# Three more pairs of up projections in seven products, their sums of x by way of DRAM, and no pair held across the two phases

## Chip, core and metric

One core of a Trainium2 chip. The metric is the device time of one execution in microseconds; the kernel before took 696.33 us as the median of three runs (696.13 to 696.6).

## What is computed

One block of an encoder on x of 512 positions by 1024 features, all in float32. The part that matters here is the channel mixer at its end; ahead of it stand a projection, a gated convolution, attention over 8 heads, and their merge through two gates and w_o, which gives a new x.

```python
h = rms_norm(x, norm_ffn_g[l])
up = causal_dwconv(h @ w_up[l], conv_ffn_w[l])      # 1024 -> 2 x 2816, three taps
a, b = jnp.split(up, 2, axis=-1)
x = x + (jax.nn.silu(a) * b) @ w_down[l]            # 2816 -> 1024
...
return rms_norm(x, norm_f_g)
```

## The kernel before

**Layout.** Features lie on the partitions and the 512 positions along the free axis, so x is 8 blocks of 128 x 512. The 2816 hidden features are 22 blocks; block j of a and block j of b are together pair j (blocks up 2j and 2j + 1 of `wup`).

**Products.** Each float32 operand is split into a high part and the remainder (`wh`, `wl` of a weight, `xh`, `xl` of an activation), and a product is three matmuls: high by high, low by high, high by low (`mm3`, L308; `passes`, L326, in an order of its own: first all that need only `wh`, then those with `wl`). Every matmul of the mixer takes 128 x 128 weights and 256 columns. The split of a chunk of weights is `split` (L274 on ScalarE makes `wh`, L278 on VectorE makes `wl`); there are two buffers of each, so the split of a chunk can begin when TensorE has finished the chunk before the current one.

**Two by two steps.** Some products are done on 2 x 2 arrangements of 128 x 128 weight blocks and of 256-column halves of two activation blocks, with seven products in place of eight (`PROD`, `seven`). The seven need sums of the weight blocks and sums of the activation blocks, and their results are put together by additions. A step handles two such arrangements and has two chunks of weights: P (blocks as they are, 768 columns, 18 matmuls) and F (four sums, 1024 columns, 24 matmuls). The sums of weights are made in DRAM: `make_forms` lists copies on SyncE's queue and adding transfers on GpSimd's queue, and `slot()`, called at places in the program, issues those whose turn it is. The forms for a group are made some 20 us ahead.

**Where they are used.** The gates (`GATES`), three up pairs (`SUP = (1, 2, 5)`), and the down projection (`STEPS`). For the up pairs, `up_forms(q)` makes the sums of two blocks of x in a single buffer `y` (four arrays of 128 x 256): `scale` (L1048, L1051, L1052), `sums` (L1055, L1056), `parts_of` (L1059, L1060), which splits y into slots 26 to 41 of `gh` and `gl`. This runs during the eight blocks of w_o (L1079 to L1081), whose squares GpSimd adds up in `ssq` (L1002); TensorE takes `ssq` (`pc_n`, L343) in the middle of the first up blocks.

**Phases.** The mixer runs in two phases (`PHASES`): up pairs 0 to 11 and a down stage of 12 steps, then up pairs 12 to 21 and a down stage of 8 steps with a rest done plainly. A plain up block is one chunk of 1024 columns and 48 matmuls. `up` evacuates it by a scaling (L1141), three taps (L561, L562, L565) and, per pair, `glu`: Silu (L1201), a product on GpSimd (L1206 for even pairs, L1213 for odd ones), then for two pairs together sums (L1223 to L1228) and splits (L1232, L1233) into `gh` and `gl`. A pair of seven products is put together by `merge` (L1162 to L1184) ahead of the taps, a pair of output blocks by `combine` (L1252 to L1271). In phase 0's down stage output pairs 0, 1 and 3 are combined; pair 2 stays open in four PSUM banks (`HELD = 2`) through phase 1's up stage, whose plain blocks therefore take turns in the other four.

**Order.** Matmuls, DMA issues and GpSimd's products stand in program order. The additions, scalings and splits of activations wait in a list (`later`) and are let out behind each split of weights, each with a cost and a due chunk (`run_later`), or are forced where something needs a bank or an operand (`flush`). Raw weights are loaded up to seven chunks ahead by SyncE's queue (`load`, four buffers for `raw`, four for F chunks).

Of the kernel before, what the change touches and what calls it, by code (L numbers as in the profile page):

```python
# [13 lines left out]
P = 128  # L14
# [39 lines left out]
HELD = 2  # L54
# [11 lines left out]
N0 = len(GATES) + len(UPD)  # L66
GROUPS = {"gate": (2, 4, 1), "up": (2, 4, 1), 0: (2, 4, 1), 1: (2, 3, 1)}
# [3 lines left out]
def block_kernel(ctx, tc, xT, vecs, wv, win, wmix, wo, wup, wst, wdp, outT):  # L71
# [70 lines left out]
    for ph, (j0, j1) in enumerate(PHASES):  # L142
        for j in range(j0, j1):
            if j in SUP:
# [45 lines left out]
    def make_forms(n0, n1, key):  # L190

        size, step, shift = GROUPS[key]
        make_forms.slot = 0
# [4 lines left out]
        for g, (a, b) in enumerate(zip(cuts, cuts[1:])):  # L198
# [15 lines left out]
            todo_bg.extend((make_forms.slot + step * k + shift * g, op) for k, op in enumerate(ops))  # L214
# [571 lines left out]
    def seven(doubles, n0, sets, operand, goes_on=None, stays=None, done=None, of="q"):  # L786
# [14 lines left out]
        for n, (name, prods) in enumerate(todo):  # L801
            wh, wl = chunk(name)
# [4 lines left out]
            for c, i, (xh, xl), b, h in prods:  # L807
                if i not in open_:
# [5 lines left out]
                    (i, b) not in before and i != goes_on, (i, b) not in after and i != stays,  # L814
                ))
            passes(out, len(out))
            if name[0] == "F":
                for i in sorted({i for _, i, *_ in prods}):
                    if (i, 0) not in after and i != stays:
                        done(i, open_.pop(i), sets[i])  # L820
# [125 lines left out]
    make_forms(len(GATES), N0, "up")  # L946
# [92 lines left out]
    def up_forms(q):  # L1039

        y = gx.tile([P, 4, 2 * P], F32, tag="y", name=f"y{q}")
        b11, b12, b21, b22 = (y[:, i, :] for i in range(4))
        fs = slice(XF + 4 * q, XF + 4 * q + 4)
# [13 lines left out]

        def parts_of():
            nc.scalar.activation(gh[:, fs, :], y, AF.Copy)  # L1059
# [5 lines left out]
    def up_form(q, g):  # L1065
# [3 lines left out]
        n = XF + 4 * q + (0, 3, 1, 2)[g - 3]  # L1069
# [3 lines left out]
    make_forms(N0, N0 + len(STEPS[0]), 0)  # L1073
    for j in range(KB):
# [11 lines left out]
        if j % 2:  # L1086
            up_forms(j // 2)
# [20 lines left out]
    USETS = {1: (2, 3, 4, 5), 2: (6, 7, 0, 1), 5: (6, 7, 0, 1)}  # L1108
    ssq3 = xp.tile([P, S], F32, tag="ssq", name="ssq3")

    def place(ph, q):
        return (q - PHASES[ph][0] // 2) * (NF + ph)

    def up(j, ph, rb2, pu=None):
# [6 lines left out]

        if j in SUP:
            c = len(GATES) + 2 * SUP.index(j)
            slot()
            seven(
                UPD[c - len(GATES) :][:2], c, {j: USETS[j]}, up_form, of="x",
# [166 lines left out]
    for ph, (j0, j1) in enumerate(PHASES):  # L1293
        if ph:
            flush()
            acc = turns(*X * 5)
        if ph:
            make_forms(N0 + len(STEPS[0]), len(DOUBLES), ph)
        for j in range(j0, j1):
# [11 lines left out]
            up(j, ph, nrm["b"], pu)  # L1311
        assert not todo_bg
        flush((("e",),))
        seven(
            STEPS[ph], N0 + ph * len(STEPS[0]), ({0: X, 1: Y, 3: X, 2: Y}, {0: X, 1: Y, 2: Y})[ph],
            lambda q, g: (gh[:, place(ph, q) + g, :], gl[:, place(ph, q) + g, :]),
            goes_on=HELD if ph == 1 else None, stays=HELD if ph == 0 else None,
            done=lambda i, banks, ids: combine(ph, i, banks, ids),
        )
# [95 lines left out]
def _layout(i):  # L1415
# [46 lines left out]
    for w4, d in [(wga, d) for d in GATES] + [(wu4, d) for d in UPD] + [(wdn, d) for d in STEPS[0] + STEPS[1]]:  # L1462
# [45 lines left out]
```

## Time and profile before

| | |
|---|---|
| median of 3 runs | 696.33 us (696.13 to 696.6) |
| profiled execution | 695.75 us, of which the span from the first to the last instruction is 693.9 us |
| mean granted TensorE clock | 0.998 |
| SyncE's and ScalarE's DMA (q1 and q10) | 42016 packets, 100.87 MB |
| GpSimd's DMA (q0) | 16304 packets, 22.88 MB |

Times in a row of the profile are microseconds from the span's start. PE is TensorE, PEld its weight loads, DVE VectorE, ACT ScalarE, POOL GpSimd, SPq SyncE's DMA queue. A row of the timeline reads: start, length, engine, line, operation, output and inputs, shape, count, and in brackets the engine's idle time before it with what ended it. A row of the groups by line gives count, busy time and the mean of one in ns. A row of waits gives the sum, the number and the longest. An operation that follows another on the same engine can begin a little before the other's end; the distance between starts is what it costs in a row of work.

### The profile page before, as it was taken

How to read it: one execution, taken by the hardware profiler on the slowest of the kernel's cores; microseconds unless marked ns; L12 is line 12 of the kernel's file. 1: busy time of each engine (PE TensorE's matmuls, PEld its weight loads, DVE VectorE, ACT ScalarE, POOL GpSimd, SP SyncE). 2: the span in 40 equal slices, each digit the busy share in tenths (PEclk: the TensorE clock that was granted, in tenths of full speed). 3: DMA queues.
4: the chain of work that ended last, by engine and by line, in shares of the span. 5: the costliest groups of instructions: out<-in, count | busy, mean ns of one | idle time of the engine just before them, and what ended most of it. 6: DMA issues, size and time to landing. Idle time of an engine off the chain costs nothing.

```text
span 693.9 us, 14635 instructions
## 1 busy us (share of the span) xinstructions
PE 686.2 (99%) x5972; PEld 684.6 (99%) x5972; DVE 531.4 (77%) x826; ACT 359.2 (52%) x565; POOL 178.3 (26%) x194
## 2 busy tenths in 40 slices
PE   9999999999999999999999999999999999999996
PEld 9999999999999999999999999999999999999996
DVE  6677877776577778768879799888774677777894
ACT  5665655644565444446554455545443344445572
POOL 4134846532221201113513134210000313222000
PEclk9999999999999999999999999999999999999999
DMA  7528988543698596766899776355646686776513
GB/s 256 158 70 272 197 200 193 129 91 92 223 263 244 166 269 193 207 217 141 114 316 294 201 178 135 116 177 176 201 128 232 141 195 157 188 169 172 164 31 122
DMA packets 58387, 124.68 MB, mean 180 GB/s; under 512 B 5280, under 2 KB 26800, under 8 KB 58320
## 3 DMA queue, kind: packets, MB, share of 16 engines
q1 hardware_dynamic: 40776, 99.68, 44.5%
q0 software_dynamic: 16304, 22.88, 20.9%
q10 hardware_dynamic: 1240, 1.19, 0.5%
q8 instruction: 47, 0.77, 0.4%
q14 instruction: 20, 0.16, 0.1%
HBM read 121.57 MB, written 39.32 MB: 232 GB/s over the span
## 4 chain that ended last, share of the span: by engine, by line
PE 96%; DVE 3%; issue 0%; ACT 0%; DVEq 0%
PE dn L326 24%; PE p_up L308 21%; PE p_in L308 14%; PE p_up L326 6%; PE p_wo L308 6%; PE yc L308 3%; PE ya L308 3%; PE pa L472 2%; PE pb L474 2%; PE p_q L308 2%; PE p_k L308 2%; PE p_gb L308 2%; PE p_ga L308 2%; PE o L653 2%; PE tp L636 1%; PE pdB L308 1%
## 5 line engine op out<-in xcount | busy, mean ns | idle before, releaser
L308 PE MATMUL p_up<-x1h,wh_up 128*128 128x256 f32 x464 | 90.5, 276 | 0.0
L308 PE MATMUL p_up<-x1h,wl_up 128*128 128x256 f32 x464 | 90.4, 276 | 0.0
L308 PE MATMUL p_up<-x1l,wh_up 128*128 128x256 f32 x464 | 90.3, 276 | 0.0
L308 PEld LDWEIGHTS p_up<-x1h,wh_up 128*128 128x128 f32 x464 | 69.9, 188 | 0.0
L308 PEld LDWEIGHTS p_up<-x1h,wl_up 128*128 128x128 f32 x464 | 69.9, 188 | 0.0
L308 PEld LDWEIGHTS p_up<-x1l,wh_up 128*128 128x128 f32 x464 | 69.8, 188 | 0.0
L274 ACT ACTIVATE wh_up<-raw_up 128x1024 fp32r<-128x1024 f32 x38 | 40.2, 1057 | 49.6 <-PE p_up L308 43.0
L210 POOL DMA_DIRECT2D f<-in_wst_dram x57 | 65.5, 1309 | 0.1
L278 DVE TENSOR_TENSOR wl_F<-raw_F,wh_F 128x1024 fp32r<-128x1024 f32 (+1 forms) x36 | 47.8, 1328 | 18.5 <-ACT wh_F L274 18.2
L308 PE MATMUL p_in<-xgh,wh_in 128*128 128x256 f32 x288 | 56.8, 279 | 0.0
L308 PE MATMUL p_in<-xgh,wl_in 128*128 128x256 f32 x288 | 56.6, 278 | 0.0
L308 PE MATMUL p_in<-xgl,wh_in 128*128 128x256 f32 x288 | 56.5, 278 | 0.0
L278 DVE TENSOR_TENSOR wl_up<-raw_up,wh_up 128x1024 fp32r<-128x1024 f32 x38 | 47.1, 1240 | 12.1 <-ACT wh_up L274 12.1
L274 ACT ACTIVATE wh_F<-raw_F 128x1024 fp32r<-128x1024 f32 (+1 forms) x36 | 37.9, 1053 | 35.4 <-PE dn L326 27.8
L1206 POOL TENSOR_TENSOR ge<-fu,fu 128x512 f32<-128x512 f32 x11 | 18.8, 1706 | 141.6 <-DVE fu L565 117.6
L274 ACT ACTIVATE wh_P<-raw_P 128x768 fp32r<-128x768 f32 (+1 forms) x36 | 30.0, 834 | 31.6 <-PE dn L326 22.3
L278 DVE TENSOR_TENSOR wl_P<-raw_P,wh_P 128x768 fp32r<-128x768 f32 (+1 forms) x36 | 35.0, 972 | 13.7 <-ACT wh_P L274 9.1
L308 PEld LDWEIGHTS p_in<-xgh,wh_in 128*128 128x128 f32 x288 | 44.7, 188 | 0.7
L326 PE MATMUL dn<-gl,wh_F 128*128 128x256 f32 x192 | 45.1, 276 | 0.0
L326 PE MATMUL dn<-gh,wh_F 128*128 128x256 f32 x192 | 45.1, 276 | 0.0
L308 PEld LDWEIGHTS p_in<-xgl,wh_in 128*128 128x128 f32 x288 | 43.7, 188 | 0.0
L308 PEld LDWEIGHTS p_in<-xgh,wl_in 128*128 128x128 f32 x288 | 43.6, 188 | 0.0
(349 smaller groups left out, 2148.5 us busy)
## 6 DMA issues: line engine op xcount, KB each, us to landing
raw_up<-in_wup_dram SPq DMA_DIRECT2D x38, 512.0 KB, 4.2
raw_F<-f SPq DMA_DIRECT2D x35, 512.0 KB, 4.5
raw_P<-in_wst_dram SPq DMA_DIRECT2D x35, 384.0 KB, 4.9
raw_in<-in_win_dram SPq DMA_DIRECT2D x26, 512.0 KB, 3.5
f<-in_wst_dram POOLq DMA_DIRECT2D x35, 256.0 KB, 6.4
f<-in_wst_dram SPq DMA_DIRECT2D x17, 512.0 KB, 5.7
f<-in_wst_dram POOLq DMA_DIRECT2D x17, 512.0 KB, 8.0
f<-f SPq DMA_DIRECT2D x34, 256.0 KB, 5.4
```

The source lines that it names most:

```text
L210: return lambda: keep(nc.gpsimd.dma_start(dst, src, accum_op=ALU.add))
L274: ins = nc.scalar.activation(hi, raw, AF.Copy)
L278: ins = nc.vector.tensor_sub(lo, raw, hi.bitcast(F32))
L308: keep(nc.tensor.matmul(out[:, cs], w, x[:, cs], start=start and i == 0 and c == 0, stop=stop and i == 2 and c == len(cut) - 1,))
L326: keep(nc.tensor.matmul(out, wl if x == 1 else wh, xl if x == 2 else xh, start=opens and bk not in seen, stop=closes and bk not in left,))
L472: keep(nc.tensor.matmul(pa[t][:, :VW], xt, w[:, VB:], start=start, stop=stop))
L474: keep(nc.tensor.matmul(pb[t], xt, w[:, :VB], start=start and t % 2 == 0, stop=stop and t % 2 == 1))
L636: keep(nc.tensor.transpose(tp[:, ks], pt[:, ks], ident))
L653: keep(nc.tensor.matmul(o[:, 2 * P * e + c0 : 2 * P * (e + 1)], w, x[:, kb, c0:], start=e == 0 and kb == 0 and i == 0, stop=e == 1 and kb ...
L1206: keep(nc.gpsimd.tensor_mul(ge, a.rearrange(halves_of, h=2), b.rearrange(halves_of, h=2)))
```

## The change

Pairs 14, 16 and 18 of phase 1 are done in seven products as well. `SUP`, `UPD` and `XF` become lists by phase. The sums of x for them are the same as those for pairs 1, 2 and 5, but their slots of `gh` and `gl` are used by other data in between: so `parts_of` stores each `y` to a DRAM array `ys` on ScalarE's queue in phase 0, and `up_forms(q, 1)` loads it again on SyncE's queue into the same single buffer and splits it a second time, one q behind each split from the last but one chunk of phase 0's down stage on, into slots 0 to 15. The places of phase 1's products in `gh` and `gl` move to leave these slots free. The sums of weights for the three pairs are listed from slot 20 on beside those of the down stage, and `seven` calls `slot()` in the down stage too. Pair 2 is no longer held: it is combined in both phases, and phase 1's plain blocks and pairs of seven products use all eight banks.

```diff
-SUP = (1, 2, 5)
-XF = 26
-UPD = tuple(((j, q), (j, q + 1)) for j in SUP for q in (0, 2))
-DOUBLES = GATES + UPD + STEPS[0] + STEPS[1]
+SUP = ((1, 2, 5), (14, 16, 18))
+XF = (26, 0)
+UPD = tuple(tuple(((j, q), (j, q + 1)) for j in js for q in (0, 2)) for js in SUP)
+DOUBLES = GATES + UPD[0] + STEPS[0] + UPD[1] + STEPS[1]
+NU = [len(GATES), len(GATES + UPD[0] + STEPS[0])]
+ND = [NU[i] + len(UPD[i]) for i in range(2)]
...
-    def seven(doubles, n0, sets, operand, goes_on=None, stays=None, done=None, of="q"):
+    def seven(doubles, n0, sets, operand, done=None, of="q", tick=False):
...
+            if tick and name[0] == "P":
+                slot()
...
-                    (i, b) not in before and i != goes_on, (i, b) not in after and i != stays,
+                    (i, b) not in before, (i, b) not in after,
...
-    def up_forms(q):
-
-        y = gx.tile([P, 4, 2 * P], F32, tag="y", name=f"y{q}")
+    ys = dr.tile([4, P, 4, 2 * P], F32, tag="ys", name="ys")
+
+    def up_forms(q, ph):
+
+        y = gx.tile([P, 4, 2 * P], F32, tag="y", name=f"y{ph}{q}")
...
         def parts_of():
             nc.scalar.activation(gh[:, fs, :], y, AF.Copy)
+            if not ph:
+                keep(nc.scalar.dma_start(ys[q], y))
             nc.vector.tensor_sub(gl[:, fs, :], y, gh.bitcast(F32)[:, fs, :])
-
+            if ph and q < 3:
+                up_forms(q + 1, ph)
+
+        if ph:
+            keep(nc.sync.dma_start(y, ys[q]))
+            due = [c[0] for c in stream].index(f"F{ND[0] + len(STEPS[0]) - 2}") + q
+            later.append((due, 0.85, (("x", q),), parts_of))
+            return
...
-    make_forms(N0, N0 + len(STEPS[0]), 0)
+    make_forms(ND[0], ND[0] + len(STEPS[0]), 0)
+    make_forms(NU[1], ND[1], "up1", 20)
...
-    USETS = {1: (2, 3, 4, 5), 2: (6, 7, 0, 1), 5: (6, 7, 0, 1)}
+    USETS = dict.fromkeys(SUP[1], (2, 3, 4, 5)) | {1: (2, 3, 4, 5), 2: (6, 7, 0, 1), 5: (6, 7, 0, 1)}
...
     def place(ph, q):
-        return (q - PHASES[ph][0] // 2) * (NF + ph)
+        return (16, 24, 32, 0, 8)[q - PHASES[1][0] // 2] if ph else q * NF
...
         if ph:
-            flush()
-            acc = turns(*X * 5)
-        if ph:
-            make_forms(N0 + len(STEPS[0]), len(DOUBLES), ph)
+            acc = turns(6, 7, 0, 1, 6, 7, 0, 1, 6, 7, 0, 1, 6, 7)
+            make_forms(ND[1], len(DOUBLES), ph)
...
             up(j, ph, nrm["b"], pu)
+        if not ph:
+            up_forms(0, 1)
+        flush_only((("e",),))
+        seven(
+            STEPS[ph], ND[ph], ({0: X, 1: Y, 3: X, 2: Y}, {0: X, 1: Y, 2: Y})[ph],
+            lambda q, g: (gh[:, place(ph, q) + g, :], gl[:, place(ph, q) + g, :]),
+            done=lambda i, banks, ids: combine(ph, i, banks, ids), tick=True,
+        )
         assert not todo_bg
```

The lines of the changed kernel are shifted by one at `split` (L279 is the L278 of before) and by 16 in `up` and `glu` (L1157 is L1141). Three places in the order of instructions matter. The first is ScalarE at the end of the blocks of w_o, from the split of the third y on; before it reads:

```order
L1059 ACTIVATE gh<-y_4392 128x1024
L274 ACTIVATE wh_up_4537<-raw_up_4331 128x1024
L1080 ACTIVATE x1h<-x_3803,vec 128x512
L1001 ACTIVATE sq_6_4460<-x_3803 128x512
L1048 ACTIVATE y_4525<-x_3803,vec 128x512
L274 ACTIVATE wh_up_4551<-raw_up_4394 128x1024
L1080 ACTIVATE x1h<-x_3803,vec 128x512
L1001 ACTIVATE sq_7_4522<-x_3803 128x512
```

and now:

```order
L1065 ACTIVATE gh<-y_4398 128x1024
L1067 DMA ys<-y_4398 128x1024
L275 ACTIVATE wh_up_4544<-raw_up_4337 128x1024
L1096 ACTIVATE x1h<-x_3803,vec 128x512
L1004 ACTIVATE sq_6_4467<-x_3803 128x512
L1053 ACTIVATE y_4532<-x_3803,vec 128x512
L275 ACTIVATE wh_up_4558<-raw_up_4400 128x1024
L1096 ACTIVATE x1h<-x_3803,vec 128x512
L1004 ACTIVATE sq_7_4529<-x_3803 128x512
```

Only the store is new; the scaling that writes the next y stands behind it in the queue and uses the buffer that it reads. VectorE's order in this stretch is unchanged.

The second is VectorE where phase 1's up stage ends and its down stage begins; wl_P and wl_F are the low parts of the first step's two chunks, fz the scalings of the last up blocks, go and gl the sums and splits of earlier pairs. Before:

```order
L1141 TENSOR_TENSOR fz_8139<-p_up_8090,rb_n_4669 128x512
L278 TENSOR_TENSOR wl_P_8212<-raw_P_8007,wh_P_8211 128x768
L562 SCALAR_TENSOR_TENSOR fu_8141<-fz_8139,vec,fu_8141 128x511
L565 SCALAR_TENSOR_TENSOR fu_8141<-fz_8139,vec,fu_8141 128x510
L1141 TENSOR_TENSOR fz_8215<-p_up_8158,rb_n_4669 128x512
L278 TENSOR_TENSOR wl_F_8245<-raw_F_8009,wh_F_8244 128x1024
```

Now, from the fourth instruction behind wl_P on (a tap, a scaling and a tap stand between):

```order
L1239 TENSOR_TENSOR go_8205<-ge_8004 128x256
L563 SCALAR_TENSOR_TENSOR fu_8281<-fz_8279,vec,fu_8281 128x511
L1240 TENSOR_TENSOR go_8205<-go_8205,ge_8004 128x256
L566 SCALAR_TENSOR_TENSOR fu_8281<-fz_8279,vec,fu_8281 128x510
L1243 SCALAR_TENSOR_TENSOR go_8205<-go_8205 128x256
L1157 TENSOR_TENSOR fz_8285<-p_up_8215,rb_n_4677 128x512
L1244 SCALAR_TENSOR_TENSOR go_8205<-go_8205 128x256
L1249 TENSOR_TENSOR gl<-ge_8004,gh 128x2x256
L1249 TENSOR_TENSOR gl<-go_8205,gh 128x512
L563 SCALAR_TENSOR_TENSOR fu_8287<-fz_8285,vec,fu_8287 128x511
L279 TENSOR_TENSOR wl_F_8331<-raw_F_8058,wh_F_8330 128x1024
```

Between wl_P and wl_F stood three instructions; now thirteen, since work of the blocks before has moved back to here.

The third is VectorE in pair 14, the first in seven products. Before, no such pair stood there. Now, from the split of its second P chunk on:

```order
L279 TENSOR_TENSOR wl_P_7258<-raw_P_7061,wh_P_7257 128x768
L1240 TENSOR_TENSOR go_7191<-go_7191,ge_7058 128x256
L1243 SCALAR_TENSOR_TENSOR go_7191<-go_7191 128x256
L1249 TENSOR_TENSOR gl<-ge_7058,gh 128x2x256
L1244 SCALAR_TENSOR_TENSOR go_7191<-go_7191 128x256
L279 TENSOR_TENSOR wl_F_7288<-raw_F_7063,wh_F_7287 128x1024
L1249 TENSOR_TENSOR gl<-go_7191,gh 128x512
L279 TENSOR_TENSOR wl_up_7318<-raw_up_7128,wh_up_7317 128x1024
```

The sum L1240 needs GpSimd's product of pair 13, and the low part of the second F chunk stands behind it.

More of the change, by code (lines that the diff above doesn't have):

```diff
@@ L53 @@
 )
-HELD = 2
 GJ = 3
@@ L188, in block_kernel, with make_forms @@
     made, todo_bg = {}, []
-    def make_forms(n0, n1, key):
+    def make_forms(n0, n1, key, start=0):
         size, step, shift = GROUPS[key]
-        make_forms.slot = 0
+        if not start:
+            make_forms.slot = 0
         cuts = [n0]
@@ L818, in seven @@
                 for i in sorted({i for _, i, *_ in prods}):
-                    if (i, 0) not in after and i != stays:
+                    if (i, 0) not in after:
                         done(i, open_.pop(i), sets[i])
```

32 lines of the change are left out of this document (12 added, 20 removed).

## Prediction

> **What bounds the kernel now.** The page comes first: its head line, the busy line, and the shares of the chain that ended last.
>
> ```profile
> span 693.9 us, 14635 instructions
> PE 686.2 (99%) x5972; PEld 684.6 (99%) x5972; DVE 531.4 (77%) x826; ACT 359.2 (52%) x565; POOL 178.3 (26%) x194
> PE 96%; DVE 3%; issue 0%; ACT 0%; DVEq 0%
> ```
>
> TensorE is busy 99% of the span and 96% of the chain is its own work. The list of waits says how much it waits once the first loads are in:
>
> ```profile
> PE p_up L326 <- DVE wl_up L278: 0.6, 1, 0.6
> ```
>
> So there is one wait of 0.6 us for VectorE, and the time is the number of matmuls times their spacing, as long as VectorE, ScalarE and the queues keep up. The chain in order of time gives the spacing:
>
> ```profile
> 468.15 57.12 PE dn L326 x504
> ...
> 526.63 4.08 PE p_up L308 x36
> ...
> 634.07 35.91 PE dn L326 x315
> ```
>
> 57.12 us over 504 matmuls is 0.1133 us each, and 4.08 over 36 is the same. The first row is the down stage of phase 0, which ends at 525.27. Phase 1's 20 up blocks run until 634.07; its down stage begins there. The profiled execution took 695.75 us around a span of 693.9; the median of the runs is 696.33, 0.58 above, so differences found in the span are put on the median.
>
> **The gain.** A plain pair is 2 blocks of 48 matmuls, 96; in seven products it is 84. Three pairs lose 36 matmuls of the same form: 36 x 0.1133 = **4.08 us**, all on the path. No other matmul is removed or added. What follows is what the new work puts in front of TensorE.
>
> **The stores of the sums (L1067 of the changed kernel).** ScalarE issues each store behind the split of y; since y has one buffer, the scaling of the next y now waits until the store has landed. Behind it in ScalarE's queue stand the next weight split, x1h and the square, and VectorE's sums of y wait for it too. This is the last of the three places, on ScalarE, VectorE, GpSimd and TensorE:
>
> ```profile
> 333.57 1.06 ACT L1059 ACTIVATE gh<-y 128x1024 fp32r<-128x1024 f32 x1 [2.35 <-DVE y L1056]
> 334.53 1.05 ACT L274 ACTIVATE wh_up<-raw_up 128x1024 fp32r<-128x1024 f32 x1
> ...
> 337.68 0.71 ACT L1048 ACTIVATE y<-x,vec 128x512 f32<-128x512 f32 x1
> ```
>
> ```profile
> 306.31 0.42 DVE L1051 TENSOR_TENSOR y<-y 128x256 f32<-128x256 f32 x1
> ...
> 338.42 1.31 DVE L1051 TENSOR_TENSOR y<-y 128x256 f32<-128x256 f32 x1
> 339.65 0.68 DVE L1079 TENSOR_TENSOR x<-p_wo,x 128x512 f32<-128x512 f32 x1
> ```
>
> ```profile
> 337.92 1.52 POOL L1002 TENSOR_TENSOR ssq<-ssq,sq 128x512 f32<-128x512 f32 x1 [4.67 <-ACT sq L1001]
> ...
> 341.75 1.52 POOL L1002 TENSOR_TENSOR ssq<-ssq,sq 128x512 f32<-128x512 f32 x1 [1.31 <-ACT sq L1001]
> ```
>
> ```profile
> 343.05 0.39 PE L308 MATMUL p_up<-x1l,wh_up 128*128 128x256 f32 x2
> 343.32 1.05 PE L343 MATMUL pc_n<-ones,ssq 128*128 128x1 f32 x8
> ```
>
> The store would issue at 334.53, the scaling starts at 337.68: 3.15 us are free. The sum of 1.31 is done in 0.42 elsewhere (306.31); it lasts until the GpSimd addition beside it is done (339.44). Without that collision it would free the queue after 0.34, so the scaling may start as late as 339.65 - 0.34 - 0.74 = 338.57, and a store may take 4.0 us before x (339.65) is late. From there nothing is spare: the addition ends at 343.27 and TensorE takes ssq at 343.32, straight behind its last matmul. A store of S us makes x late by S - 4.0, and since the next split of y is late by the same, three stores in a row cost TensorE 3 x (S - 4.0).
>
> No 512 KB store is in this trace. The nearest rows are the output's stores (128 and 256 KB), the loads of 512 KB in a quiet stretch (raw_up from 500 to 560), and those of this stage (raw_wo), in this order, as smallest, median, largest:
>
> ```profile
> DMA to landing us min/median/max: 1.7/2.9/3.7
> ```
>
> ```profile
> DMA to landing us min/median/max: 3.5/3.8/4.3
> ```
>
> ```profile
> DMA to landing us min/median/max: 4.2/5.1/6.5
> ```
>
> The ends are 0 (1.7) and 3 x 2.5 = 7.5 us (6.5). I take S = 4.2, nearer to the quiet load, since the stores stand in ScalarE's own queue and not behind SyncE's copies: **0.6 us**. The Trainium skill's page "DMA: Bandwidth & Descriptors", section "Anatomy of one DMA — SWDGE (gpsimd) path", gives about 2.0 us plus bytes over 436 GB/s, which as an estimate for 512 KB is 3.2 us; by it the stores cost nothing and the time would be 694.0. The same section says the receipt from HBM is the heavy part and can delay the signal surprisingly long, which speaks against this change; the loads here, above 3.2 in every row, bear the second sentence out better than the figure.
>
> **Loading the sums back.** The load of y1 waits for VectorE's split of y0; SyncE's queue holds it in front of y2 and of the load of up27, neither of which is needed before 536. ScalarE's split of y1 stands in front of that of the first up block:
>
> ```profile
> 514.88 1.07 ACT L274 ACTIVATE wh_F<-raw_F 128x1024 fp32r<-128x1024 f32 x1 [1.65 <-PE dn L326]
> ...
> 521.91 1.06 ACT L274 ACTIVATE wh_up<-raw_up 128x1024 fp32r<-128x1024 f32 x1 [1.20 <-PE dn L326]
> ```
>
> ```profile
> 515.98 1.23 DVE L278 TENSOR_TENSOR wl_F<-raw_F,wh_F 128x1024 fp32r<-128x1024 f32 x1 [0.41 <-ACT wh_F L274]
> ```
>
> y0's low part follows at 517.1 and ends at 518.3; the load at 3.8 lands at 522.2, ScalarE's split ends at 523.2, the block's two splits at 524.3 and 525.5. TensorE wants the low half eight matmuls after 525.27, at 526.2: 0.7 us to spare, 0.2 with a load of 4.3, and 1.3 late at 5.8. y2 and y3 go round the same way (about 6.2 us each) and come out some 1.9 us before up27 wants its split. Zero here.
>
> **VectorE in the new stage.** Back to back, its operations stand this far apart:
>
> ```profile
> 427.10 1.21 DVE L278 TENSOR_TENSOR wl_up<-raw_up,wh_up 128x1024 fp32r<-128x1024 f32 x1
> 428.23 0.74 DVE L562 SCALAR_TENSOR_TENSOR fu<-fz,vec,fu 128x511 f32<-128x511 f32 x1
> 428.89 0.41 DVE L1233 TENSOR_TENSOR gl<-ge,gh 128x256 fp32r<-128x256 f32 x1
> 429.23 0.74 DVE L565 SCALAR_TENSOR_TENSOR fu<-fz,vec,fu 128x510 f32<-128x510 f32 x1
> 429.89 0.68 DVE L1233 TENSOR_TENSOR gl<-go,gh 128x512 fp32r<-128x512 f32 x1
> 430.49 0.68 DVE L1141 TENSOR_TENSOR fz<-p_up,rb_n 128x512 f32<-128x512 f32 x1
> 431.09 1.28 DVE L1233 TENSOR_TENSOR gl<-go,gh 128x512 fp32r<-128x512 f32 x2
> ```
>
> 1.13 for 1024 columns, 0.66 for a tap, 0.60 for 512, 0.34 for 256. A plain pair is two splits, two scalings and four taps, 6.1, and half of the sums for the down stage (four of 256, four splits of 512, 3.8), 1.9: 8.0 us beside 10.88 of TensorE. A pair of seven products has splits of 768 (0.87) and 1024, twice, 4.0, merge and taps 6.1, and the 1.9: 12.0 us beside 9.52. Two such neighbours are 20.0 against 20.4, so VectorE only just holds from 14 to 19 and is behind at the end, where its order decides. Before, that end reads:
>
> ```profile
> 628.67 0.69 DVE L1141 TENSOR_TENSOR fz<-p_up,rb_n 128x512 f32<-128x512 f32 x1 [0.54 <-PE p_up L308]
> 629.55 0.96 DVE L278 TENSOR_TENSOR wl_P<-raw_P,wh_P 128x768 fp32r<-128x768 f32 x1 [0.19 <-ACT wh_P L274]
> ...
> 635.28 1.23 DVE L278 TENSOR_TENSOR wl_F<-raw_F,wh_F 128x1024 fp32r<-128x1024 f32 x1 [0.47 <-ACT wh_F L274]
> ```
>
> wl_F is ready 2.44 after the last block's end E (634.07); TensorE wants it after the P chunk's 18 matmuls and 16 of the F chunk's, at E + 3.85. Now wl_P can start at E - 4.52 as before (its buffer is freed by the last but one block), and 13 operations stand between it and wl_F: five taps, two scalings, four sums, two splits of 512, 3.30 + 1.20 + 1.36 + 1.20 = 7.06. With 0.87 for wl_P, wl_F starts at E + 3.41 and is ready at E + 4.64, **0.8 late**. Then a tap, two splits and the next wl_P (0.66 + 1.20 + 0.96) end at E + 7.36, where TensorE, resumed at 4.64, wants it 0.91 + 1.36 later at 6.91: **0.45 late**. After that the old slack returns.
>
> Three rows more bear on the start of the stage: VectorE's wait for the first block, its wait for GpSimd's product, and the down stage ahead of it in the table by stretches (length, then busy time and count of TensorE, its loads, VectorE, ScalarE, GpSimd, then clock, share of the DMA engines and GB/s):
>
> ```profile
> 530.75 0.69 DVE L1141 TENSOR_TENSOR fz<-p_up,rb_n 128x512 f32<-128x512 f32 x1 [4.02 <-PE p_up L308]
> ...
> 552.51 0.43 DVE L1224 TENSOR_TENSOR go<-go,ge 128x256 f32<-128x256 f32 x1 [1.46 <-POOL go L1213]
> ```
>
> ```profile
> 468.00:525.30 57.30, 57.30 (x508) 57.30 (x507) 42.58 (x57) 27.45 (x34) 0.00 (x0) 1.00 0.59 179
> ```
>
> The seven additions of pair 2's combine and the splits of y2 and y3 go into the 4.0 us ahead of the first block and the waits that follow it. The weight sums for pairs 14, 16 and 18 end in the down stage, where GpSimd did nothing and the DMA engines were busy 59%; the loads that they feed are due 22 us later. So both cost nothing, and a late sum would show as a wait for a raw tile. The tight spots are wl_up24 (0.7), the second F chunk of pair 14, which now stands behind GpSimd's product (walked through with the spacings above it is ready 30.0 us after the stage's start and wanted at 30.4), and up30 (0.4). A collision such as the 1.31 above stretches an operation by 0.9; one that lands on a tight spot costs up to 0.5. I take **0.5** for all, ends 0 and 1.5.
>
> **Sum.** -4.08 + 0.6 + 0.8 + 0.45 + 0.5 = -1.73; 696.33 - 1.73 = **694.6 us**.
>
> **Rivals.** *Nothing waits* (chance 0.18): stores within 4.0 us, and VectorE's order a little kinder than my sum: -4.08, 692.2. For it: no wait but one in the whole trace. Against it: the 7.06 us are a plain sum of rows. *The stores are late* (0.18), which ends slower: nothing else hides a landing, and every 0.1 us above 4.0 counts three times. The gain without stores is 4.08 - 1.75 = 2.33, so they cancel it from S = 4.0 + 2.33 / 3 = 4.8 on; at 5.6, within raw_wo's rows, it is 4.8 us instead of 0.6, 698.8. GpSimd's adding transfers run beside the second and third store, for it; the separate queue, against. *VectorE is overrun* (0.12): its idle time in phase 1 goes, so GpSimd's ten products meet it; at 0.5 each on four spots more, 2 us, 696.6. The Trainium skill's page "SBUF — State Buffer", section "SBUF: two separate sides", calls that port pair an exclusive lock held for the whole instruction; the 1.31 us row agrees.
>
> **Numbers.** The forecast has 0.52, its own range 693.6 to 695.8, the rest the rivals. What a measurement of this kernel can tell is about 0.2%, 1.4 us, so faster means below 694.9: 0.36 of the forecast's share and the first rival's 0.18, 0.54. Same: 0.16 of the forecast, most of the overrun (0.12) and the store case between 4.8 and 5.2 (0.03), 0.31. Slower 0.15, the rest of the stores. The range runs from the full gain, 692.2, to 697.6 (S near 5.2), leaving out late stores beyond that.
>
> **What would show it.** TensorE's matmuls fewer by 36; the waits of TensorE: pc_n on ssq near 343 by 3 x (S - 4.0), with S read from the stores' landing; dn on wl_F and then wl_P at the start of the last down stage; a small one near pair 14. Wrong would be stores beyond 5 us, or waits of TensorE on a raw tile's load.

## The result and the profile after

The changed kernel took 704.48 us (median of 4 runs, 704.01 to 705.18) against 696.41 for the kernel before on the same chip: a ratio of 1.0118, interval 1.0103 to 1.0133. It is **8.1 us slower**, where 694.6 was predicted and 697.6 was the upper end. The profiled execution took 704.37, its span is 702.6.

The head of the page after, its busy line and its chain by engine:

```profile
span 702.6 us, 14695 instructions
PE 688.5 (98%) x5936; PEld 686.2 (98%) x5936; DVE 551.7 (79%) x858; ACT 369.8 (53%) x579; POOL 190.2 (27%) x203
PE 86%; DVE 6%; DMA 4%; ACT 2%; issue 1%; POOL 0%; DVEq 0%; SPq 0%; ACTq 0%; POOLq 0%
```

The 36 matmuls are gone (5972 to 5936), yet TensorE is busy 2.3 us longer: single matmuls must have become slower. And the chain, which was 96% TensorE's own work, now runs through VectorE, DMAs and ScalarE. The list of TensorE's waits names where (sum, number, longest):

```profile
PE dn L327 <- DVE wl_F L279: 2.9, 2, 2.5
PE pc_n L344 <- POOL ssq L1005: 2.7, 1, 2.7
PE warm L115 <- DVE ones L107: 1.1, 1, 1.1
PE p_up L309 <- DVE wl_up L279: 0.6, 1, 0.6
PE p_up L327 <- DVE wl_up L279: 0.6, 1, 0.6
```

The waits for ones and one of those for wl_up were there before. New are 2.7 + 0.6 us at the first up blocks, and 2.5 + 0.4 at the last down stage and near pair 14. The table by stretches of 2 us, for both places, shows the rest. Behind the length stand busy time and count of TensorE, its loads, VectorE, ScalarE and GpSimd, then the granted clock:

```profile
346.00:348.00 2.00, 0.32 (x3) 0.32 (x3) 1.85 (x3) 0.90 (x2) 1.51 (x1) 1.00 0.82 122
348.00:350.00 2.00, 2.00 (x12) 2.00 (x12) 0.96 (x3) 1.06 (x1) 0.62 (x1) 0.55 0.73 154
350.00:352.00 2.00, 2.00 (x11) 2.00 (x11) 1.23 (x1) 0.00 (x0) 2.00 (x3) 0.50 0.78 217
352.00:354.00 2.00, 2.00 (x11) 2.00 (x11) 0.00 (x0) 0.00 (x0) 0.55 (x1) 0.50 0.82 260
354.00:356.00 2.00, 2.00 (x16) 2.00 (x15) 0.00 (x0) 0.50 (x1) 0.00 (x0) 0.74 1.04 401
642.00:644.00 2.00, 0.00 (x0) 0.00 (x0) 2.00 (x4) 1.99 (x3) 0.00 (x0) 1.00 0.00 0
644.00:646.00 2.00, 1.46 (x9) 1.46 (x10) 2.00 (x4) 2.00 (x4) 0.00 (x0) 0.79 0.19 35
646.00:648.00 2.00, 2.00 (x11) 2.00 (x11) 2.00 (x3) 0.30 (x1) 0.00 (x0) 0.50 0.57 227
648.00:650.00 2.00, 2.00 (x17) 2.00 (x16) 1.35 (x3) 0.85 (x1) 0.00 (x0) 0.86 0.50 126
```

Behind each of the two long waits TensorE is granted half its clock, for 6.8 and 3.4 us; a row of 2 us then holds 11 or 12 matmuls in place of 20. The loss is the missing share of the clock times 2 us, summed: 2 x (0.45 + 0.50 + 0.50 + 0.26) = 3.4 us and 2 x (0.21 + 0.50 + 0.14) = 1.7 us. So the span's difference of 8.7 us is -4.08 for the matmuls, +2.7 + 0.6 + 2.9 for the waits, +3.4 + 1.7 for the clock, together 7.2, and 1.5 us that the list of waits does not name (0.57 of it lies ahead of the blocks of w_o, where the change does nothing).

**The first wait** comes down ScalarE's queue. Its timeline, the splits of y and the scalings of the next y (ACTq is the issue of the store; the first two rows are the first store and the scaling behind it):

```profile
312.17 0.34 ACTq L1067 DMA_DIRECT2D ys<-y  x1
...
316.51 0.72 ACT L1053 ACTIVATE y<-x,vec 128x512 f32<-128x512 f32 x1 [0.17 <-DMA ys<-y]
...
323.16 0.33 ACTq L1067 DMA_DIRECT2D ys<-y  x1
...
329.95 0.72 ACT L1053 ACTIVATE y<-x,vec 128x512 f32<-128x512 f32 x1 [2.61 <-DMA ys<-y]
...
336.00 1.06 ACT L1065 ACTIVATE gh<-y 128x1024 fp32r<-128x1024 f32 x1 [2.37 <-DVE y L1061]
336.03 0.33 ACTq L1067 DMA_DIRECT2D ys<-y  x1
...
342.91 0.72 ACT L1053 ACTIVATE y<-x,vec 128x512 f32<-128x512 f32 x1 [2.71 <-DMA ys<-y]
```

The last two of these scalings start 6.8 and 6.9 us behind the issue of the store, and the engine sat idle 2.6 and 2.7 us for it; the first starts 4.3 us behind, and ScalarE sat idle 0.17. The store is issued while ScalarE's split of y begins (336.03, 336.00), not behind it. From there it goes on as the prediction had it: VectorE's x of the last block, GpSimd's addition, TensorE:

```profile
344.01 0.68 DVE L1095 TENSOR_TENSOR x<-p_wo,x 128x512 f32<-128x512 f32 x1
```

```profile
346.12 1.51 POOL L1005 TENSOR_TENSOR ssq<-ssq,sq 128x512 f32<-128x512 f32 x1 [3.24 <-ACT sq L1004]
```

```profile
347.68 1.42 PE L344 MATMUL pc_n<-ones,ssq 128*128 128x1 f32 x8 [2.72 <-POOL ssq L1005]
```

x stood at 339.65 before, the addition at 341.75, pc_n at 343.32: all are 4.4 us late.

**The second wait** is that of the first F chunk of the last down stage. VectorE's splits and the two long taps between, and GpSimd at the same time:

```profile
632.11 1.50 DVE L563 SCALAR_TENSOR_TENSOR fu<-fz,vec,fu 128x511 f32<-128x511 f32 x1
634.31 0.95 DVE L279 TENSOR_TENSOR wl_P<-raw_P,wh_P 128x768 fp32r<-128x768 f32 x1
635.18 0.74 DVE L563 SCALAR_TENSOR_TENSOR fu<-fz,vec,fu 128x511 f32<-128x511 f32 x1
637.43 1.78 DVE L563 SCALAR_TENSOR_TENSOR fu<-fz,vec,fu 128x511 f32<-128x511 f32 x1
...
643.27 1.22 DVE L279 TENSOR_TENSOR wl_F<-raw_F,wh_F 128x1024 fp32r<-128x1024 f32 x1
```

```profile
631.76 1.30 POOL L1229 TENSOR_TENSOR go<-fu,fu 128x512 f32<-128x512 f32 x1 [8.60 <-ACT fu L562]
637.32 1.34 POOL L1222 TENSOR_TENSOR ge<-fu,fu 128x512 f32<-128x512 f32 x1 [4.26 <-ACT fu L562]
```

A tap takes 0.74 alone, and 1.50 and 1.78 while GpSimd multiplies.

### The profile page after: what moved, and what is told of

Read it like the earlier page. It is cut to its first block, busy times and chain, and to the rows that moved or that the text cites. A ratio compares the mean times of both kernels' runs of the same rounds, so it can differ in the third digit from the quotient of the medians.

```text
span 702.6 us, 14695 instructions
## 1 busy us (share of the span) xinstructions
PE 688.5 (98%) x5936; PEld 686.2 (98%) x5936; DVE 551.7 (79%) x858; ACT 369.8 (53%) x579; POOL 190.2 (27%) x203
## 4 chain that ended last, share of the span: by engine, by line
PE 86%; DVE 6%; DMA 4%; ACT 2%; issue 1%; POOL 0%; DVEq 0%; SPq 0%; ACTq 0%; POOLq 0%
PE dn L327 26%; PE p_up L309 15%; PE p_in L309 14%; PE p_up L327 5%; PE yc L309 3%; PE ya L309 3%; DMA ys<-y 3%; PE pa L473 2%; PE pb L475 2%; PE p_q L309 2%; PE p_k L309 2%; PE p_gb L309 2%; PE p_ga L309 2%; PE o L654 2%; PE tp L637 1%; PE p_wo L309 1%
## 5 line engine op out<-in xcount | busy, mean ns | idle before, releaser
L211 POOL DMA_DIRECT2D f<-in_wst_dram x66 | 75.1, 1389 | 31.6 <-DMA f<-f 31.6
L309 PE MATMUL p_up<-x1h,wl_up 128*128 128x256 f32 x392 | 77.5, 280 | 0.6 <-DVE wl_up L279 0.6
L309 PE MATMUL p_up<-x1h,wh_up 128*128 128x256 f32 x392 | 77.7, 280 | 0.0
L309 PE MATMUL p_up<-x1l,wh_up 128*128 128x256 f32 x392 | 77.3, 279 | 0.0
L279 DVE TENSOR_TENSOR wl_F<-raw_F,wh_F 128x1024 fp32r<-128x1024 f32 (+1 forms) x42 | 55.1, 1313 | 19.3 <-ACT wh_F L275 19.3
L309 PEld LDWEIGHTS p_up<-x1h,wl_up 128*128 128x128 f32 x392 | 60.1, 191 | 0.8 <-DVE wl_up L279 0.8
L309 PEld LDWEIGHTS p_up<-x1h,wh_up 128*128 128x128 f32 x392 | 60.3, 191 | 0.0
L309 PEld LDWEIGHTS p_up<-x1l,wh_up 128*128 128x128 f32 x392 | 60.0, 191 | 0.0
L279 DVE TENSOR_TENSOR wl_P<-raw_P,wh_P 128x768 fp32r<-128x768 f32 (+1 forms) x42 | 40.8, 971 | 17.0 <-ACT wh_P L275 12.5
L327 PE MATMUL dn<-gh,wh_F 128*128 128x256 f32 x228 | 53.8, 276 | 0.0
L327 PE MATMUL dn<-gl,wh_F 128*128 128x256 f32 x228 | 53.8, 276 | 0.0
L279 DVE TENSOR_TENSOR wl_up<-raw_up,wh_up 128x1024 fp32r<-128x1024 f32 x32 | 40.9, 1278 | 6.5 <-ACT wh_up L275 6.3
```

Source lines behind the costliest of these rows:

```text
L211: return lambda: keep(nc.gpsimd.dma_start(dst, src, accum_op=ALU.add))
L279: ins = nc.vector.tensor_sub(lo, raw, hi.bitcast(F32))
L309: keep(nc.tensor.matmul(out[:, cs], w, x[:, cs], start=start and i == 0 and c == 0, stop=stop and i == 2 and c == len(cut) - 1,))
L327: keep(nc.tensor.matmul(out, wl if x == 1 else wh, xl if x == 2 else xh, start=opens and bk not in seen, stop=closes and bk not in left,))
```

## The experiments

The theory behind the first runs has three parts. A: the stores' landing, through the single buffer, costs the wait for ssq. B: VectorE is behind at the last down stage because of the third pair. C: an idle TensorE loses its clock, which doubles the price of both. The rivals are that the stores hurt by their traffic, that the wait at the end lies in the order of instructions and not in their number, and that the clock falls for another reason. The results, each as a ratio to the kernel before on the same chip:

| kernel | us | ratio, 95% interval |
|---|---|---|
| a_two_y | 697.27 | 1.0016 (1.0007 to 1.0026) |
| a_early | 705.17 | 1.0125 (1.0107 to 1.0143) |
| a_fill | 700.59 | 1.0064 (1.0049 to 1.0079) |
| b_stores | 702.88 | 1.0096 (1.0080 to 1.0111) |
| a2_budget | 702.46 | 1.0088 (1.0074 to 1.0101) |
| a2_pairs | 696.69 | 1.0014 (1.0005 to 1.0023) |
| b_slow1 | 699.03 | 1.0048 (1.0033 to 1.0063) |
| b_slow2 | 701.90 | 1.0085 (1.0072 to 1.0099) |
| a3_split | 697.69 | 1.0019 (1.0010 to 1.0028) |
| a3_split2 | 697.09 | 1.0015 (1.0006 to 1.0025) |
| a4_tbl | 694.13 | 0.9972 (0.9961 to 0.9984) |
| a2_dve2 | 696.43 | 1.0007 (0.9998 to 1.0016) |

### The stores: a_two_y and b_stores

The changed kernel with a second place for y (a_two_y):

```diff
-        y = gx.tile([P, 4, 2 * P], F32, tag="y", name=f"y{ph}{q}")
+        pool = gx if ph or q % 2 else hp
+        y = pool.tile([P, 4, 2 * P], F32, tag="y", name=f"y{ph}{q}")
```

> The changed kernel, with the sums of x for the even q in a second buffer, so that a scaling waits for the store before the last and no longer for the last one. Theory A (the stores' landing is what delays the chain from the scaling of y to ssq; TensorE then waits 2.7 us for ssq and 0.6 us for a weight split, and runs at half clock for some 7 us behind it): both waits go, the clock stays at 1.0 near 350, and the time falls from 704.5 by 2.7 + 0.6 + 3.5 = 6.8 us to about 697.7 (697 to 698.5). Rival (the stores delay the stage by their traffic, whatever buffer they read): the waits stay, 702 to 705.

The kernel before with the stores and nothing else (b_stores):

```diff
             nc.scalar.activation(gh[:, fs, :], y, AF.Copy)
+            keep(nc.scalar.dma_start(ys[q], y))
```

> The kernel before with nothing but the four stores of y added on ScalarE's queue; nobody reads what they store. Theory A: the stores alone bring the wait of 2.7 us for ssq, some 0.5 us for a split, and 3.5 us at half clock: 696.4 + 6.7 = about 703 (702 to 704). Rival (the loss at the start comes from other work that the change brings there, such as the longer list of weight sums): under 698.

Both came out as theory A said: 697.27 (expected 697.7) and 702.88 (expected 703). In a_two_y no scaling waits for a store any more, pc_n starts at 343.33 as before the change, and the table by stretches keeps the full clock:

```profile
346.00:348.00 2.00, 2.00 (x20) 2.00 (x19) 0.89 (x1) 0.02 (x1) 1.83 (x2) 1.00 0.83 197
348.00:350.00 2.00, 2.00 (x20) 2.00 (x19) 0.96 (x1) 0.83 (x1) 0.00 (x0) 1.00 1.00 390
```

The same four stores move the same bytes there, and the slowest of the transfers of ys even takes longer to land than in the changed kernel (longest 8.2 us, against 6.8). So TensorE waits because of the buffer and not because of the traffic. In b_stores, where ys is only stored, the view of that tile gives the landing without the loads among it (smallest, median, largest):

```profile
DMA to landing us min/median/max: 6.7/6.8/6.8
```

The view can tell the landing of two of the four stores only, the second and the third. The first was quicker: the scaling behind it starts 4.1 us after its issue (311.56, 315.64) and waits for nothing. What makes the difference is not shown. In the changed kernel GpSimd issues one of its adding transfers 1.4 us ahead of the second store and again ahead of the third (321.79 and 334.66) and none near the first, and the DMA engines are busy 0.68 of the stretch from the first store's issue to its landing, 0.95 and 0.87 of the other two; no run takes these transfers away.

### The clock: a_fill, b_slow1 and b_slow2

The changed kernel with idle multiplications put into the two waits (a_fill):

```diff
+    def filler(b, n):
+        t = bank(b, "fill")
+        for _ in range(n):
+            keep(nc.tensor.matmul(t[:, :P], ones, ones, start=True, stop=True))
...
                 def mid():
+                    filler(7, 11)
                     nrm["c"] =
...
-            passes(out, len(out))
+            passes(out, len(out), 10 if name == f"F{ND[1]}" else 0)
```

> The changed kernel with multiplications added whose results nobody reads: 11 matmuls of 128 columns ahead of pc_n and 10 ahead of the first that needs wl_F in the last down stage, each about 0.21 us by the first matmuls of the trace (4.21 us for 9 at half clock), so 2.3 and 2.1 us of work inside waits of 2.7 and 2.5. Theory C (the clock falls because TensorE stands idle in these two waits, and the half clock costs 3.5 and 2 us more): the granted clock stays at 1.0 in both places, the waits are filled but nothing starts earlier, and the time falls by 4.5 to 5.5 us to about 699.5. Rival (the clock falls for another cause, such as the load of the chip, or the waits alone are the loss): the clock falls as before and the time stays within 1 us of 704.5.

The kernel before with one or two operations more ahead of pc_n (b_slow1, b_slow2):

```diff
+    for _ in range(NSLOW):
+        nc.gpsimd.tensor_scalar(ssq2, ssq2, 1.0, None, op0=ALU.mult)
     hg.close()
```

> The kernel before with one more GpSimd operation of 128x512 on ssq (times 1.0), so that TensorE must wait some 1.3 us for ssq. If the clock falls with any wait: 1.3 us and some 3.5 us at half clock, 701. If a wait must be longer than this for the clock to fall: 696.3 + 1.3 = 697.6, with a granted clock of 1.0 behind it.

> The kernel before with two more GpSimd operations of 128x512 on ssq (times 1.0), so that TensorE waits some 2.7 us for ssq, with no store and no transfer added. Theory C (the idle time of TensorE alone brings the clock down): half clock for some 7 us behind the wait, 696.3 + 2.7 + 3.5 = 702.5. Rival (the stores or the load of the DMA engines near 350 bring it down): the clock stays at 1.0, 699.0.

In a_fill the work needed starts no earlier than in the changed kernel, and the time falls by 3.9 us (expected 4.5 to 5.5). TensorE's rows at the two places show the fill and what is left of the waits, and the last one a wait that the slow clock had covered:

```profile
345.19 2.72 PE L318 MATMUL fill<-ones 128*128 128x128 f32 x22
348.13 1.05 PE L352 MATMUL pc_n<-ones,ssq 128*128 128x1 f32 x8 [0.22 <-POOL ssq L1013]
...
639.32 2.39 PE L318 MATMUL fill<-ones 128*128 128x128 f32 x20
642.02 1.21 PE L335 MATMUL dn<-gh,wl_F 128*128 128x256 f32 x8 [0.30 <-DVE wl_F L279]
644.75 0.97 PE L335 MATMUL dn<-gh,wl_P 128*128 128x256 f32 x6 [0.16 <-DVE wl_P L279]
```

The granted clock is 1.00 throughout both places. So the clock is the second half of the price, and an idle TensorE is the reason. The two slowed kernels say how long idle must last. b_slow1, the wait and the stretch behind it:

```profile
345.54 1.05 PE L344 MATMUL pc_n<-ones,ssq 128*128 128x1 f32 x8 [1.53 <-POOL ssq L1090]
```

```profile
348.00:350.00 2.00, 2.00 (x20) 2.00 (x20) 0.00 (x0) 0.00 (x0) 2.00 (x3) 1.00 0.98 385
```

and b_slow2:

```profile
347.13 1.86 PE L344 MATMUL pc_n<-ones,ssq 128*128 128x1 f32 x8 [3.11 <-POOL ssq L1090]
```

```profile
348.00:350.00 2.00, 2.00 (x10) 2.00 (x11) 0.97 (x2) 0.00 (x0) 0.72 (x1) 0.50 0.95 387
```

A wait of 3.1 us with no store near halves the clock; b_slow2 took 701.9 (expected 702.5). A wait of 1.5 us leaves it at 1.00 in the profiled execution, which took 697.97 and fits the 697.6 of a wait alone. But the five executions of b_slow1 reach from 697.65 to 701.2, and their mean clocks from 0.998 down to 0.994: at this length it falls in some executions and not in others.

How long it stays down follows a pattern. The loss, summed over rows of 2 us as above, is 3.4 us behind the first wait of the changed kernel, the first of a_early, and those of b_slow2 and a2_budget; it is 1.7 us behind the second wait of the changed kernel and of a_early, and behind those of a_two_y, b_stores and a2_dve2. So half clock lasted 6.8 us or 3.4, and behind these waits no other length was seen. Nor does it begin with the wait: in b_stores TensorE works again from 347.14, has the full clock until 348, and 0.87 and 0.50 in the next two rows. That profiled execution, at 701.45 the fastest of four, lost 1.7 us and not the 3.5 that was expected; the two slowest, at 703.62 and 703.75, have mean clocks of 0.993 where it has 0.996. The four times of b_slow2 lie in two pairs 1.7 us apart (700.91 and 701.16, 702.64 and 702.89), which fits one such length or two, though only one of them was profiled.

### The end: a_early, a2_pairs and a2_budget

One number in the list of pairs (a_early), or one pair fewer (a2_pairs, on a_two_y):

```diff
-SUP = ((1, 2, 5), (14, 16, 18))
+SUP = ((1, 2, 5), (13, 15, 17))
```

```diff
-SUP = ((1, 2, 5), (14, 16, 18))
+SUP = ((1, 2, 5), (14, 16))
...
-            acc = turns(6, 7, 0, 1, 6, 7, 0, 1, 6, 7, 0, 1, 6, 7)
+            acc = turns(*X * 4)
```

> The changed kernel with pairs 13, 15 and 17 in place of 14, 16 and 18, so that four plain pairs and not three stand between the last pair of seven products and the down stage. Theory B (VectorE is behind at the start of the last down stage because the heavy pairs end too near to it; 2.9 us of waits for wl_F and wl_P and some 4 us at half clock come from that): the plain pair more gives VectorE 2.9 us, the wait for wl_F falls from 2.5 to below 0.3 us, and the time falls by 4.5 to 5 us, to about 699.7 (699 to 701). Rival (the wait only moves: the first such pair stands 11 us nearer to the loads of y and the weight sums, and TensorE waits there): 702.5 or more, with a wait of TensorE near pair 13.

> The kernel with two buffers for y, and with pairs 14 and 16 alone in seven products (pair 18 plain again). Both theories of the end expect no wait of TensorE there: 24 matmuls fewer than before, 24 x 0.1133 = 2.7 us, so 693.6 (693.2 to 694.5). A wait for wl_F of over 1 us here would speak against both, and for a cause at the end itself that does not come from the number of such pairs.

And larger sums for the work that is let out behind each split (a2_budget, on a_two_y):

```diff
-            run_later(k, {"u": 4.2, "P": 1.6, "F": 1.2}[nm[0]])
+            run_later(k, {"u": 4.8, "P": 2.0, "F": 2.0}[nm[0]])
```

> The kernel with two buffers for y, and larger sums of postponed work let out behind each split while products of the seven are pending (4.8, 2.0, 2.0 in place of 4.2, 1.6, 1.2). Theory B2 (VectorE has the time, but its order postpones the scalings and taps of the up blocks until they stand between wl_P and wl_F at the end): only 6 to 8 operations stand there now, the waits of 2.9 us and the 4 us at half clock behind them go, and the full gain of 4.08 us is left: 696.3 - 4.1 = 692.2, at most 693.5. Rival (VectorE is full from pair 14 on, by its own work and by GpSimd's products, so that any order only moves the wait): 695 or more, with waits of TensorE for a weight split between 560 and 630.

a_early and a2_budget missed what their theories expected by far, and in the same way. The rivals had the time in their range (702.5 or more, 695 or more) but not the wait that made it: a_early has 0.7 us near its first pair of seven products, a2_budget none for a weight split between 560 and 630. TensorE's waits of a_early and of a2_budget, one row of each:

```profile
PE dn L327 <- ACT wh_F L275: 4.0, 1, 4.0
```

```profile
PE dn L327 <- ACT wh_F L275: 3.7, 1, 3.7
```

The wait is now for the *high* part, which ScalarE makes. ScalarE's timeline in a2_budget shows why:

```profile
635.59 0.63 ACT L1218 ACTIVATE fu<-fu 128x512 f32<-128x512 f32 x1 [1.16 <-DVE fu L566]
636.24 1.28 ACT L1220 ACT_TABLE_LOAD   x1
637.53 0.29 ACT L1220 ACTIVATE tbl<-fu,ex 32x1 f32<-32x1 f32 x1
637.73 0.70 ACT L562 ACTIVATE fu<-fz,vec 128x512 f32<-128x512 f32 x1
638.35 1.04 ACT L275 ACTIVATE wh_F<-raw_F 128x1024 fp32r<-128x1024 f32 x1
```

wh_F could start when the last up block ends (about 633.5), but stands in the queue behind a Silu that waits for VectorE, the load of the table for the square root, and the last block's tap. So the number of operations between wl_P and wl_F was not the whole of it: ScalarE's order, too, comes out of how far the last block's evacuation has been postponed. In a2_budget the larger sums also hold in phase 0, where TensorE's waits for wl_up grow from 0.6 to 1.7 us. a2_pairs did better (696.69), but not the 693.6 that 24 matmuls fewer give: its waits of 0.8, 0.6, 0.4 and 0.6 us for wh_P, wh_F, wl_F and wl_up (the last is in the kernel before as well) take back 1.8 of the 2.7, but its span is 0.5 longer than before (694.4, 693.9), so some 1.4 us stay unexplained.

### The end again: a3_split, a3_split2 and a4_tbl

The larger sums in phase 1 alone, and the split of the first F chunk ahead of the last block's evacuation (a3_split; a3_split2 with other sums):

```diff
+            two = k > [c[0] for c in stream].index(f"F{ND[0] + len(STEPS[0]) - 1}")
+            run_later(k, ({"u": 4.2, "P": 1.6, "F": 1.2}, {"u": 4.8, "P": 2.0, "F": 2.0})[two][nm[0]])
...
             if i and j + 1 == PHASES[ph][1]:
                 split_next()
+                if ph:
+                    split()
...
-                    f()
+                    with after_split() if ph and i and j + 1 == NP else ExitStack():
+                        f()
```

> Two buffers for y, the larger sums of postponed work (4.8, 2.0, 2.0) in phase 1 alone, and the split of the first F chunk of the last down stage placed ahead of the evacuation of the last up block, on ScalarE and on VectorE. Theory E (a2_budget lost its time because wh_F stood on ScalarE behind that evacuation's Silu, table load and tap, which wait for VectorE; VectorE itself has the time): the wait of 3.7 us for wh_F and the half clock behind it go, wl_F stands 5 operations behind wl_P, and 36 matmuls fewer remain as the gain: 695.8 - 4.1 + up to 1 of small stalls = 692 to 693.5. Rival (VectorE is full, the work that is moved behind wl_F makes the next wl_P or the sums of the last pairs late): a wait of over 1 us at the next chunks, 694.5 or more.

> As a3_split with 5.2, 2.0, 1.6 in place of 4.8, 2.0, 2.0: more behind each plain split and less behind each F split. Theory E expects the same time within 0.7 us, since the order at the end is the same; the rival expects the waits of TensorE in the up stage of phase 1 to differ by what the heavier plain splits delay.

Here the rival seemed to win: no wait for wh_F, no lost clock, but 697.69 and 697.09, with two new waits. TensorE in a3_split:

```profile
638.19 0.38 PE L328 MATMUL dn<-gh,wh_P 128*128 128x256 f32 x1 [1.30 <-ACT wh_P L275]
650.73 0.38 PE L328 MATMUL dn<-gl,wh_P 128*128 128x256 f32 x1 [1.36 <-DVE gl L1254]
```

Both still had a place in the program: the table load now stood ahead of the second wh_P, and the last pairs' sums had become due one chunk later, since their due times count from the split that had been moved. a4_tbl mends these two and nothing else:

```diff
         if j == NP - 1:
-            nc.scalar.activation(tbl, a[: 4 * H, :1], AF.Sqrt, scale=0.0, bias=eps[: 4 * H])
+            k -= 1
...
+        if j == NP - 1:
+            later.append((k + 7, 0, (("t", 0),), lambda: nc.scalar.activation(
+                tbl, gh.bitcast(F32)[: 4 * H, g0, :1], AF.Sqrt, scale=0.0, bias=eps[: 4 * H])))
```

> As a3_split2, with ScalarE's table load for the square root moved behind the splits of the last two pairs (it stood ahead of the second wh_P of the last down stage, which came 1.0 to 1.3 us late), and with the last pairs' product and sums due one chunk earlier, as before the change (their last split came 1.4 us late). Theory F (VectorE has the time for three such pairs; what was left were these two orders): both waits go, 697.1 - 1.0 - 1.4 = 694.7 (693.7 to 695.2), with no wait of TensorE over 0.6 us in the last down stage. Rival (VectorE is full, and each order moves the wait on): another wait of 1 to 3 us in the last down stage, 696 to 698.

It took 694.13, 1.9 us less than the kernel before, and its list of waits ends like this:

```profile
PE warm L115 <- DVE ones L107: 1.1, 1, 1.1
PE p_up L328 <- DVE wl_up L279: 0.6, 1, 0.6
PE dn L328 <- DVE wl_F L279: 0.4, 1, 0.4
```

The rival falls: with VectorE's work the same, all waits at the last down stage are gone. What was wrong there was the order, on VectorE and on ScalarE. This is the version that beats both kernels. It does not get the whole 4.08: TensorE's last matmuls start at 684.85 in place of 687.42, 2.6 us earlier. In the up stage of phase 1 a wait of 0.35 and about 1 us of small stalls are lost, and 0.7 us behind the last matmul; the reason for the latter stays open.

### GpSimd beside VectorE: a2_dve2

The products of pairs 19 and 20 on VectorE, on a_two_y:

```diff
-            keep(nc.gpsimd.tensor_mul(ge, a.rearrange(halves_of, h=2), b.rearrange(halves_of, h=2)))
+            mul = nc.vector.tensor_mul if j == 20 else nc.gpsimd.tensor_mul
...
+            if j == 19:
+                mul(nc.vector)
```

> The kernel with two buffers for y, and the products of pairs 19 and 20 on VectorE in place of GpSimd, each at 0.6 us of VectorE's row; all other operations of VectorE keep their order. In that kernel the tap beside the first product took 1.49 us and the one beside the second 1.79, where a tap alone takes 0.74. Theory G (the two taps were stretched because GpSimd worked beside them, which is the difference between the 0.8 us that was predicted for wl_F and the 2.5 us that were measured): no tap over 0.8 us there, wl_F starts 8.5 us behind wl_P and no longer 9.0, both products together give back 0.75 + 1.05 - 1.2 = 0.6 us, and the wait for wl_F is 1.9 us. If the clock still falls behind a wait of 1.9 us, about 696.7; if it does not, about 694.7. Rival (the taps wait for their input and GpSimd is only beside them): they stay as long, the wait grows by 1.2 us, 698 or more.

As expected: 696.43, the wait for wl_F 2.0 us in place of 2.5 (expected 1.9), every tap 0.75 at most, and wl_F starts 8.5 us behind wl_P. So the two stretched taps came from GpSimd, at 0.75 + 1.05 us. The eleven executions reach from 695.49 (mean clock 0.998) to 698.38 (0.996); a wait of 2.0 us, again, brings the clock down in some only (in the profiled one, at 697.22, it fell).

## Why the prediction was wrong, step by step

In the span, the profiled execution is 8.7 us longer where 1.7 less was forecast, a miss of 10.4 us: 5.1 of lost clock, 2.7 more at the stores than the 0.6 of the sum, 1.3 more at the start of the last down stage than its 0.8 + 0.45, and 1.5 that no wait names, less 0.15 near pair 14.

**The gain** of 36 x 0.1133 = 4.08 us is real: 36 matmuls fewer, and a kernel whose other parts are in order is faster than before.

**The stores** had the right mechanism and the wrong size. The prediction had the path from the landing through scaling, x, GpSimd's addition to pc_n, the slack of 4.0 us, the price of every 0.1 us counted three times, and named "stores beyond 5 us" as what would be wrong. S was taken as 4.2. The first scaling that needed a landing started 4.3 us behind the store's issue (312.17, 316.51), the next two 6.8 and 6.9; the fourth store holds nobody. By its own formula that gives 0.3 + 2.8 + 2.8 = 5.9 us, within the range of 0 to 7.5 that it stated for the cost. pc_n came 4.4 us late, of which 0.57 came from ahead of the blocks of w_o: 3.8, so the formula was 2 us too high for that S. The reason is in the rows above: the prediction let the store issue when ScalarE's split of y has ended (334.53 in the trace of before), and it issues when that split starts (333.57 there), 1.0 us earlier. With 5.0 us of slack in place of 4.0, the first landing costs nothing and the other two 1.8 and 1.9, 3.7 together. The step that failed is S, the choice within that range: I put the store nearer to quiet loads, "since the stores stand in ScalarE's own queue and not behind SyncE's copies". A queue of its own did not make it quick; raw_wo's loads of the same stretch, at most 6.5, were the better neighbour. At 4.2 the stores would have cost nothing. The estimate of 3.2 us from the Trainium skill's page "DMA: Bandwidth & Descriptors", section "Anatomy of one DMA — SWDGE (gpsimd) path", is less than half of the 6.8; that section is on GpSimd's path, and the store stands in ScalarE's queue. Its sentence that the receipt from HBM can be late fits better, though no run here tells receipt from queueing, and the loads that the prediction called as witnesses for it do not write to DRAM.

**The clock** was not in the sum at all, neither as a term nor as a rival; this is the larger error, and the step of the prediction that failed most: each wait was priced at its length. The traces put 3.4 and 1.7 us of half clock behind two waits of 2.5 to 2.7 us, 5.1 of the 8.7. In the middle of the kernel before nothing shows it: with no wait above 0.6 us, its clock is 1.00 until the tail. At the start there is a sign: the first matmuls (`warm`, L115) are 18 records in 4.21 us, 0.23 us each, where the 22 of the same shape in a_fill's first wait take 2.72, 0.12 each.

**The start of the last down stage** was found in the right place, by the right count of operations between wl_P and wl_F, at 0.8 us. It was 2.5, because two taps were stretched by 1.8 us by GpSimd's products. The prediction had this collision in another row (1.31 us) and in its rival of an overrun VectorE, but put it at 0.5 us for all the tight spots together. The second term, 0.45 for wl_P, did not show: at half clock TensorE wants wl_P later. It appears as 0.16 in a_fill, where the clock stays up.

**Loading the sums back, the weight sums and the banks** cost nothing that a wait shows, as predicted; there is no wait for a raw tile, and the small one near pair 14 is 0.35 us.

**The rivals.** "The stores are late" was the right one, at a chance of 0.18 and 698.8 us; S was beyond the 5.6 at which it was priced, and with half clock behind it b_stores alone is at 702.9. That its 4.8 us are near the 3.8 by which pc_n was late is luck: S was taken too short and the slack too short, and the two cancel in part.

## What to carry to other kernels

A store added behind an engine's work is a wait for its landing as soon as the next writer shares its buffer; give the buffer a second place before counting on slack. On a TensorE that is otherwise never idle, price a wait of 1.5 us or more at its length plus the clock that it may cost, here 1.7 or 3.4 us, and prefer to fill it. Where a list puts work off, look at the end of a stage, on every engine in the chain: what was put off stands there, in front of the next stage's first operands.

## What the runs showed of the chip that was not expected

- TensorE's granted clock falls to 0.50 after it has been idle 2.5 us and more in every profiled execution with such a wait (the changed kernel and a_early twice each, a_two_y, b_stores, b_slow2, a2_budget), and only in some executions after 1.5 and 2.0 us. Even 2.5 us may not do it every time: two of a_two_y's ten executions, at 696.13 and 696.52 us, have mean clocks of 0.997 and 0.998 where the others have 0.995 or 0.996. It stays down for 3.4 or 6.8 us. The Trainium skill's page "TensorE: Matmul & The Clock Gate", section "HAM oscillation — how this bites in real kernels", warns of idle gaps of more than about 3.4 us; shorter ones suffice here, and the measurement decides. That its window runs free (section "Part 1: The HAM clock gate (the "warmup" mystery)") agrees with executions of one kernel that differ.
- Two 512 KB stores from ScalarE's queue landed 6.7 and 6.8 us after their issue in b_stores, and one within 4.1; the quiet loads of that size in the trace of before took 3.5 to 4.3.
- A VectorE tap of 0.74 us took 1.50 and 1.78 while GpSimd multiplied 128x512; on VectorE itself the product took 0.68.
